# One core, an mLSTM and differential-attention block: z of the odd heads and two gate blocks as three pairs with seven products each

## The chip, the core and the metric

The kernel runs on one core of a Trainium2 chip. The metric is the device time of one execution in microseconds (us), the median of several runs. PE is the engine of the matrix products (TensorE), DVE the vector engine, ACT the scalar engine, POOL is GpSimd, SP issues most DMAs.

## The reference

One layer over 1024 tokens of width 1024, all in float32. The input is normed (h), then projected with one wide matrix `w_in` into twelve segments:

```python
h = rmsnorm(x, norm_g[layer])
proj = jnp.einsum('bsd,de->bse', h, w_in[layer])
(a_q, a_k, a_v, a_o, a_z, a_g, b_q, b_k, b_v, b_z, g_a, g_b) = jnp.split(proj, _split_points(), axis=-1)
...
y_a = hm * jax.nn.sigmoid(a_o) * jax.nn.silu(a_z)
...
att = diff_attention(dq, dk, da_v, lam)
att = rmsnorm(att, da_subln_g[layer]) * (1.0 - lambda_init)
y_b = att.reshape(B, S, DA_WIDTH).astype(x.dtype) * jax.nn.silu(b_z)
...
mix = (jax.nn.sigmoid(g_a + gb[0]) * jnp.einsum('bsc,cd->bsd', y_a, w_branch_a[layer])
       + jax.nn.sigmoid(g_b + gb[1]) * jnp.einsum('bsc,cd->bsd', y_b, w_branch_b[layer]))
x = x + jnp.einsum('bsd,de->bse', mix, w_out[layer])
```

Branch A is a gated linear recurrence in chunks, in both directions, with 4 heads (hm). Branch B is attention with 8 heads; each head has two score matrices, softmaxes both, and takes one from the other times lambda. `b_z` has 128 columns for each head of branch B; `g_a` and `g_b` have 8 blocks of 128 columns each.

## The kernel before

Every float32 product is made of three passes: both operands are split into a high and a low part (names that end in H and L, `wH`, `wL`, `hH`, `hL`), and H*H, H*L and L*H are summed in PSUM.

The stages, in order of time: the start (norm, transposes of x, four blocks of gates with plain projections), to 68 us; the **pair stage**, to 398 us; the lead-in to attention (q and k of head 0, its z, and the values of heads 0 and 1), to 455 us; **attention** of 8 heads, to about 1120 us; branch A's recurrence (the ML stage); the last gates; the two branch products, the mix and the output.

*A plain projection* (`proj`, L415) takes a block of 128 columns of `w_in` and makes it for 1024 tokens in two halves of 512. Each half is 24 matmuls of 128x512 (8 blocks of the inner dimension, three passes), cut into 8 pieces of 3. One block is 48 matmuls.

*A pair* (`pair_units`, L270) makes two blocks of 128 columns for all tokens as a 2x2 product of halves with seven products (named f = 0 to 6) in place of eight. Each product is 4 inner blocks by three passes, 12 matmuls, so a pair has 84. `load_form` (L230) makes the seven weight forms from the two raw blocks: sums and differences on POOL (L243, L254), the H part on ACT (L262), the L part on DVE for f = 0, 4, 6 and on POOL for the others (L264). The operands of the other side (`TH`, `TL`) are made once and live until the stage ends. Three products share one PSUM bank, and ACT copies partial sums out of it (`u`, L298) before the next may be added. A *sink* takes the four results. There are 16 pairs: in groups of four, a pair of `ak` (with the convolution), one of `ao` and `az`, one of `aq` (convolution), one of `ao` and `az`. Raw blocks lie by turns in the pool of weights (even pairs) and in the stage's own pool (odd pairs). Work of branch A's scalar gates and of the rope tables is put in at fixed pairs (`more`).

*A head of attention* has 8 steps (`da_cycle`), a step being 128 query rows. Names below are tiles: score products `S` (12 matmuls of 64 rows, two score matrices, one PSUM buffer each); on DVE the two maxima `nm` (L926); on ACT the two exponentials `e` (L928); on DVE `r` and the combination `e` (L932 to L934). The result is transposed a step later, in two groups of four (`T`), copied as `pH` by ACT (L947) and `pL` by DVE (L948). Every second step has `PV`, 24 matmuls with the values, whose result ACT copies out as `att` (L961), and the other steps have the transposes of `att` for the squares. In steps 4 and 5 the head before is finished (`G`, L991): its `att` times z (`zg`) is scaled and stored. The transposes, PV, the squares and G share two PSUM buffers (tag `T`).

Into these steps other work is woven: the plain projections of q and k of the next head, with rope (`da_proj`, L842: `first` and `second`, DVE products, POOL sums and casts, then DMAs that spread the halves into `kst` and `qq`), the values of the next two heads (`da_v`), z of a head, and gate blocks (`fill`; how many for each head is in `FILL`, L38). The order is written by `Weaver` (L62) from costs and lags in a table (`LAG`, L42); PE then runs in that order, and the other engines in one that the framework's scheduler sets.

z of head h is 48 matmuls, a tanh on ACT (L880) and a product on DVE (L881). Of the 16 gate blocks 4 run at the start, 1 in head 0, 3 in head 7, 3 behind head 7, 2 in the ML stage, 3 after it.

Of the kernel before, what the change touches and what calls it, by code (L numbers as in the profile page):

```python
# [7 lines left out]
F32 = mybir.dt.float32  # L8
F32R = mybir.dt.float32r
I32 = mybir.dt.int32  # L10
AF = mybir.ActivationFunctionType
ALU = mybir.AluOpType
AX = mybir.AxisListType

S = 1024
# [3 lines left out]
NH_B = 8  # L19
# [15 lines left out]


INF = 1.0e9
FILL = (1, 0, 0, 0, 0, 0, 0, 3)  # L38
MM = 0.214
TP = 0.109  # L40

# [68 lines left out]
class Block:  # L110
# [202 lines left out]
    def oz_sink(self, i0):  # L313


        v, a, box = self.v, self.a, {}

        def sink(i, j, ps, rest):
            if "z" not in box:
                box["z"] = self.big("oz")  # L320
            z = box["z"][:, j * 512:(j + 1) * 512]
            first = j not in box
            box[j] = True
            if rest is not None:
                to = self.psA.tile([128, 512], F32, name="pj", tag="pj", bufs=2) if i == j == 1 else ps
                v.tensor_tensor(out=to, in0=ps, in1=rest, op=ALU.add)
                ps = to
            more = lambda out, x, y: v.scalar_tensor_tensor(out=out, in0=x, scalar=1.0, in1=y, op0=ALU.add, op1=ALU.mult)
            if i == 0:
                a.activation(out=z if first else ps, in_=ps, func=AF.Tanh, scale=0.5)  # L330
                if not first:
                    more(z, ps, z)
            else:
                th = self.s0.tile([128, 512], F32, name="tz", tag="tz", bufs=2)
                a.activation(out=th, in_=ps, func=AF.Tanh, scale=0.5)
                more(z if first else ps, th, ps)
                if not first:
                    more(z, z, ps)
            if not first:
                self.q.dma_start(out=self.gd_ml[i0][:, j * 512:(j + 1) * 512], in_=z)  # L340
        return sink

    def conv_sink(self, seg, n):

# [497 lines left out]
    def da_proj(self, h, st):  # L842
        A, v, a, p, q = self.A, self.v, self.a, self.p, self.q
        w1 = self.w1
        fb = lambda x: x.bitcast(F32)
        kA, kB = ("rope", h, 0), ("rope", h, 1)

        def first(half, pa):
            c = slice(half * 512, (half + 1) * 512)
            m = [w1.tile([128, 512], F32, name=f"m{i}", tag=f"m{i}", bufs=1) for i in range(2)]  # L850
            st["m"] = m
            v.tensor_tensor(out=m[0], in0=pa, in1=self.cosT[:, c], op=ALU.mult)
            v.tensor_tensor(out=m[1], in0=pa, in1=self.sinT[:, c], op=ALU.mult)

        def second(half, pb):
            c = slice(half * 512, (half + 1) * 512)
            if half == 0:
                st["k"] = w1.tile([128, 2, S], F32R, name="kst", tag="kst", bufs=2)
            qq = st["q", half] = w1.tile([128, 2, 512], F32R, name="qq", tag="qq", bufs=3)
            m = st["m"]  # L860

            hl = w1.tile([128, 4, 512], F32R, name="hl", tag="hl", bufs=1)
            v.tensor_tensor(out=fb(hl[:, 2]), in0=pb, in1=self.sinT[:, c], op=ALU.mult)
            v.tensor_tensor(out=fb(hl[:, 3]), in0=pb, in1=self.cosT[:, c], op=ALU.mult)
            p.tensor_tensor(out=m[0], in0=m[0], in1=fb(hl[:, 2]), op=ALU.subtract)
            p.tensor_tensor(out=m[1], in0=fb(hl[:, 3]), in1=m[1], op=ALU.add)
            for i in range(2):
                p.tensor_copy(hl[:, i, :], m[i])
                p.tensor_tensor(out=hl[:, 2 + i, :], in0=m[i], in1=fb(hl[:, i, :]), op=ALU.subtract)
            for x in range(2):  # L870
                for i, to in enumerate((st["k"][:, :, c], qq)):
                    for j in range(2):
                        r, g = 64 * j + 32 * x, 64 * (1 - i) + 32 * j
                        q.dma_start(out=fb(to[r:r + 32]), in_=fb(hl[g:g + 32, x::2]))

        kz = ("w_in", OFF["bz"] + 128 * h)

        def zz(half, ps):
            st["g", half] = g = w1.tile([128, 512], F32, name="zg", tag="zg", bufs=2)
            a.activation(out=g, in_=ps, func=AF.Tanh, scale=0.5)  # L880
            v.scalar_tensor_tensor(out=g, in0=g, scalar=1.0, in1=ps, op0=ALU.add, op1=ALU.mult)  # L881

        qk = []
        for half in range(2):
            qk += self.proj(kA, half, lambda ps, half=half: first(half, ps))
            qk += self.proj(kB, half, lambda ps, half=half: second(half, ps), name=("qk", h))
        z = self.proj(kz, 0, lambda ps: zz(0, ps)) + self.proj(kz, 1, lambda ps: zz(1, ps), name=("z", h))
        for half in range(2):
            z[(half + 1) * self.PIECES - 1].after = ((("G", h - 1, half), LAG["G"]),)
        return qk, z  # L890
# [538 lines left out]
    def build(self):  # L1429
# [19 lines left out]
        do = lambda f, cost=0.0: Unit(cost, f)  # L1449
        pool = lambda *x, **k: tc.tile_pool(*x, **k)  # L1450
        with pool(name="const", bufs=1) as self.const, \
# [16 lines left out]
            dt = lambda n: [self.dram.tile([128, S], F32, name=f"{n}{i}") for i in range(8)]  # L1468
            self.tg = {"ga": dt("tga"), "gb": dt("tgb")}
            self.ya, self.yb, self.gd_ml = dt("ya"), dt("yb"), dt("gm")  # L1470
            self.cd = {n: dt("c" + n) for n in ("ak", "akH", "akL", "aqH", "aqL")}
            self.pairs, sinks, self.praws, self.f = [], [], {}, {}
            for n in range(NH_A):
                for i, seg in enumerate(("ak", "aq")):
                    self.pairs.append(((seg, 2 * n), (seg, 2 * n + 1)))
                    sinks.append(self.conv_sink(seg, n))
                    self.pairs.append((("ao", 2 * n + i), ("az", 2 * n + i)))
                    sinks.append(self.oz_sink(2 * n + i))
            self.ident = self.const.tile([128, 128], F32, name="ident")
            make_identity(self.nc, self.ident)  # L1480
            self.mhalf = self.const.tile([128, 8], F32, name="mhalf")
            self.v.memset(self.mhalf, -0.5)

            gq = [("gb", i) for i in range(8)] + [("ga", i) for i in range(8)]
            fill = lambda m: sum((self.gate_units(*gq.pop(0)) for _ in range(m)), [])

            def begin():
# [15 lines left out]
            w = Weaver()  # L1503
# [40 lines left out]
            w.add(leave("ps0", "s0", "tf"), enter("w1", "w1", side="right"), banks("ps1", S=2, T=2))  # L1544
            w.banks.update(S=1, T=2)
            qk, z = zip(*[self.da_proj(h, sts[h]) for h in range(NH_B)])
            w.add(do(lambda: setattr(self, "ahead", True)), *qk[0], *z[0], *self.da_v(0, sts[0:2]))
            prev = None
            for h in range(NH_B):
                cur = self.da_parts(h, sts[h])  # L1550
                main = sum((self.da_cycle(cur, prev, t) for t in range(8)), [])
                ahead = qk[h + 1] if h + 1 < NH_B else []
                if h + 1 == NH_B:
                    nxt = fill(FILL[h]) + z[h]
                elif h % 2 == 1:
                    nxt = ahead + self.da_v((h + 1) // 2, sts[h + 1:h + 3]) + fill(FILL[h])
                else:
                    nxt = z[h - 1] + ahead + fill(FILL[h]) + z[h] if h else ahead + fill(FILL[0])
                w.weave(main, nxt)
                prev = cur  # L1560
            end = sum((self.da_cycle(None, prev, t) for t in range(6)), [])
# [79 lines left out]
```

## Time and profile before

| | us |
|---|---|
| median of three runs | 1701.33 (1698.94 to 1702.51) |
| the profiled execution | 1699.79 |
| its span, first to last instruction | 1698.0 |
| PE busy with matmuls | 1650.1 |
| DVE, ACT, POOL busy | 994.1, 760.0, 635.3 |

The profiled execution lies 1.5 us under the median. Times of rows are counted from the start of its span. A matmul of 512 columns shows a duration of about 0.39 us in a row, but the next one starts 0.23 us after it: the matmuls overlap, and what counts is the distance of the starts.

### The profile page before, as it was taken

The page shows a single profiled execution, that of the slowest core. Times are in us where ns is not written, and L with a number is a line of the kernel's source. Part 1 is how long each engine was busy: PE and PEld are TensorE (multiplying, and loading weights), DVE is VectorE, ACT ScalarE, POOL GpSimd, SP SyncE. Part 2 cuts the span into 40 slices and gives each one's busy share as a digit, 9 for nine tenths or more (in the row PEclk, how much of TensorE's full clock was granted, in tenths as well). Part 3 has the DMA queues.
Part 4 walks back from the last instruction along what each step waited for, and adds up shares of the span by engine and source line. Part 5 has one row for each costly group of instructions (what it writes and reads, how often), then busy time and mean ns, then how long its engine had stood idle before and what let it go on. Part 6 is the DMA issues. An engine that isn't in the chain of part 4 may idle for free. (4 is left out here: it accounts for less than half of the span.)

```text
span 1698.0 us, 25367 instructions
## 1 busy us (share of the span) xinstructions
PE 1650.1 (97%) x9431; PEld 1387.7 (82%) x9431; DVE 994.1 (59%) x1799; ACT 760.0 (45%) x1522; POOL 635.3 (37%) x712
## 2 busy tenths in 40 slices
PE   7999999999999999999999999999999898999998
PEld 5777887887888988898888888889999777888887
DVE  5778668674277666766666765126666644135533
ACT  6454555543254454454445454325656644022221
POOL 5767676665343235424351431221331311212000
PEclk9999999999999999999999999999999999999999
DMA  5334434434231213221230221175554327344222
GB/s 179 101 118 134 137 115 134 124 124 137 75 81 44 63 38 87 63 63 37 76 88 26 63 75 63 50 208 155 143 170 140 104 93 244 119 142 136 87 92 83
DMA packets 175630, 178.79 MB, mean 105 GB/s; under 512 B 12185, under 2 KB 135410, under 8 KB 175506
## 3 DMA queue, kind: packets, MB, share of 16 engines
q1 hardware_dynamic: 174594, 175.58, 34.5%
q8 instruction: 74, 1.21, 0.3%
q10 hardware_dynamic: 912, 1.59, 0.2%
q14 instruction: 50, 0.41, 0.1%
HBM read 114.11 MB, written 46.24 MB: 94 GB/s over the span
## 5 line engine op out<-in xcount | busy, mean ns | idle before, releaser
L429 PE MATMUL pj<-hH,wH 128*128 128x512 f32 x640 | 266.3, 416 | 3.3 <-ACT f L542 1.5
L429 PE MATMUL pj<-hH,wL 128*128 128x512 f32 x640 | 251.9, 394 | 1.7 <-POOL wL L207 1.7
L429 PE MATMUL pj<-hL,wH 128*128 128x512 f32 x640 | 250.6, 392 | 0.2 <-DVE hL L580 0.2
L209 POOL TENSOR_TENSOR wL<-raw,wH 128x1024 fp32r<-128x1024 f32 x41 | 99.6, 2429 | 284.2 <-ACT wH L204 281.8
L928 ACT ACTIVATE e<-S,nm 128x1024 f32<-128x1024 f32 x128 | 142.7, 1115 | 134.2 <-DVE nm L926 133.9
L948 DVE TENSOR_TENSOR pL<-T,pH 128x512 fp32r<-128x512 f32 x128 | 87.9, 688 | 117.4 <-ACT pH L947 116.7
L926 DVE TENSOR_REDUCE nm<-S 128x1 f32<-128x1024 f32 x128 | 150.5, 1217 | 10.1 <-PE S L923 9.3
L429 PEld LDWEIGHTS pj<-hH,wH 128*128 128x128 f32 x640 | 120.7, 189 | 37.8 <-issue 14.4
L451 PE MATMUL pj<-wH,hH 128*128 128x256 f32 x512 | 149.9, 293 | 1.6 <-DVE vL L1035 1.3
L451 PE MATMUL pj<-wL,hH 128*128 128x256 f32 x512 | 144.9, 283 | 1.4 <-POOL wL L207 1.4
L429 PEld LDWEIGHTS pj<-hH,wL 128*128 128x128 f32 x640 | 120.4, 188 | 30.1 <-POOL wL L207 3.1
L451 PE MATMUL pj<-wH,hL 128*128 128x256 f32 x512 | 144.5, 282 | 0.0
L429 PEld LDWEIGHTS pj<-hL,wH 128*128 128x128 f32 x640 | 121.0, 189 | 18.2 <-DVE hL L580 0.6
L429 PE MATMUL pj<-sl_yb,wH 128*128 128x512 f32 x384 | 121.8, 397 | 4.7 <-ACT sl_yb L1314 2.1
L947 ACT CAST pH<-T 128x512 fp32r<-128x512 f32 x128 | 74.7, 584 | 100.5 <-PE T L131 99.9
L204 ACT CAST wH<-raw 128x1024 fp32r<-128x1024 f32 x56 | 58.8, 1050 | 126.8 <-PE pj L429 86.4
L923 PE MATMUL S<-kst,qq 64*128 64x512 f32 x768 | 106.5, 408 | 0.0
L451 PEld LDWEIGHTS pj<-wH,hH 128*128 128x128 f32 x512 | 97.7, 191 | 6.8 <-issue 3.9
L451 PEld LDWEIGHTS pj<-wL,hH 128*128 128x128 f32 x512 | 97.5, 190 | 2.3 <-POOL wL L207 2.3
L451 PEld LDWEIGHTS pj<-wH,hL 128*128 128x128 f32 x512 | 97.7, 191 | 0.1
L429 PEld LDWEIGHTS pj<-sl_yb,wH 128*128 128x128 f32 x384 | 73.3, 191 | 22.8 <-DVE sl_yb L1315 3.3
L934 DVE SCALAR_TENSOR_TENSOR e<-e,r,e 128x1024 f32<-128x1024 f32 x64 | 88.8, 1388 | 2.2
(358 smaller groups left out, 4099.9 us busy)
## 6 DMA issues: line engine op xcount, KB each, us to landing
raw<-in_w_in_dram SPq DMA_DIRECT2D x88, 512.0 KB, 3.8
kst<-hl SPq DMA_DIRECT2D x64, 128.0 KB, 2.4
qq<-hl SPq DMA_DIRECT2D x64, 128.0 KB, 2.4
x<-in_x_dram SPq DMA_DIRECT2D x8, 512.0 KB, 6.2
cak<-y SPq DMA_DIRECT2D x16, 256.0 KB, 2.3
cakH<-cin SPq DMA_DIRECT2D x16, 256.0 KB, 4.4
cakL<-tz SPq DMA_DIRECT2D x16, 256.0 KB, 4.0
gm<-oz SPq DMA_DIRECT2D x16, 256.0 KB, 2.8
```

What stands on the lines that cost most here:

```text
L204: self.a.copy(wH, raw)
L209: self.p.tensor_tensor(out=wL, in0=raw, in1=wHf, op=ALU.subtract)
L429: self.t.matmul(ps, lhsT=l[:, k, :], rhs=r, start=(n == 0), stop=(n == 23))
L451: self.t.matmul(ps[:, i, :], lhsT=l, rhs=r[:, k, :], start=(kh == 0 and k == 0 and m == 0), stop=(kh == 1 and k == 3 and m == 2))
L923: self.t.matmul(ps[:, o], lhsT=qq[r, x, c], rhs=k[r, y, o], start=(m == 0), stop=(m == 2))
L926: v.tensor_reduce(out=nm, in_=ps, axis=AX.X, op=ALU.max, negate=True)
L928: a.activation(out=e, in_=ps, func=AF.Exp, bias=nm[:, 0:1], accum_out=Z[:, j, t:t + 1])
L934: v.scalar_tensor_tensor(out=e0, in0=e, scalar=r[:, 0:1], in1=e0, op0=ALU.mult, op1=ALU.add)
L947: a.copy(pH[:, :, s], ps)
L948: v.tensor_tensor(out=pL[:, :, s], in0=ps, in1=pH[:, :, s].bitcast(F32), op=ALU.subtract)
```

## The change

Six blocks move from plain projections into pairs: z of heads 1, 3, 5 and 7 (two pairs) and the blocks 4 and 5 of branch B's gate (one pair). The new pairs stand behind the fourth pair of the groups 0, 1 and 2, so there are 19. Their sinks write z (with its tanh and product) and the gate to DRAM. In attention, an odd head loads its z from there into the same buffers `zg` (`load_z`, after the last G of the head before). Even heads keep the plain projection of z, now alone beside the next head's q and k. z of head 0 moves from the lead-in into head 0, in the place of a gate block. Head 7 has two gate blocks in place of three and its z. The cast of the rotated q and k on GpSimd, which the words for the change name, stands in the kernel before too (L868); the diff has no line of it.

```diff
-FILL = (1, 0, 0, 0, 0, 0, 0, 3)
+FILL = (0, 0, 0, 0, 0, 0, 0, 2)
...
+    def stored_sink(self, to, finish):
+        box = {}
+        def sink(i, j, ps, rest):
+            if i not in box:
+                box[i] = self.big("out")
+            out = box[i][:, j * 512:(j + 1) * 512]
+            if rest is not None:
+                sums = self.psA.tile([128, 512], F32, name="pj", tag="pj", bufs=2) if i == j == 1 else ps
+                self.v.tensor_tensor(out=sums, in0=ps, in1=rest, op=ALU.add)
+                ps = sums
+            finish(out, ps, i)
+            self.q.dma_start(out=to[i][:, j * 512:(j + 1) * 512], in_=out)
+        return sink
...
+    def z_sink(self, heads):
+        def finish(out, ps, i):
+            self.a.activation(out=out, in_=ps, func=AF.Tanh, scale=0.5)
+            self.v.scalar_tensor_tensor(out=out, in0=out, scalar=1.0, in1=ps, op0=ALU.add, op1=ALU.mult)
+        return self.stored_sink([self.gz[h] for h in heads], finish)
...
+        def load_z(half):
+            st["g", half] = g = w1.tile([128, 512], F32, name="zg", tag="zg", bufs=2)
+            q.dma_start(out=g, in_=self.gz[h][:, half * 512:(half + 1) * 512])
+
+        if h % 2 == 1:
+            return qk, [Unit(0.0, lambda half=half: load_z(half)) for half in range(2)]
...
+                if n < 3:
+                    blocks = (("gb", 4), ("gb", 5)) if n == 0 else (("bz", 4 * n - 3), ("bz", 4 * n - 1))
+                    self.pairs.append(blocks)
+                    sinks.append(self.gate_sink(blocks) if n == 0 else self.z_sink([h for _, h in blocks]))
...
-            gq = [("gb", i) for i in range(8)] + [("ga", i) for i in range(8)]
+            gq = [("gb", i) for i in (0, 1, 2, 3, 6, 7)] + [("ga", i) for i in range(8)]
...
-            w.add(do(lambda: setattr(self, "ahead", True)), *qk[0], *z[0], *self.da_v(0, sts[0:2]))
+            w.add(do(lambda: setattr(self, "ahead", True)), *qk[0], *self.da_v(0, sts[0:2]))
...
-                    nxt = fill(FILL[h]) + z[h]
+                    nxt = fill(FILL[h])
                 elif h % 2 == 1:
-                    nxt = ahead + self.da_v((h + 1) // 2, sts[h + 1:h + 3]) + fill(FILL[h])
+                    nxt = ahead + self.da_v((h + 1) // 2, sts[h + 1:h + 3])
                 else:
-                    nxt = z[h - 1] + ahead + fill(FILL[h]) + z[h] if h else ahead + fill(FILL[0])
+                    nxt = ahead + z[h]
+                if h % 2 == 1:
+
+                    k = [i for i, u in enumerate(main) if u.name and u.name[0] == "G"][-1] + 1
+                    main[k:k] = z[h]
```

(`gate_sink`, left out, is `z_sink` with the gate's tanh alone, on ACT, and the gate's tiles in DRAM.)

The first place is PE in head 7, step 6, from its score products on (`pj` are projections, `att` the squares' transposes, `e` the transposes of the probabilities). Before:

```order
L923 MATMUL S<-kst,qq 128x512 x12
L429 MATMUL pj<-hH_170,wH 128x512
L429 MATMUL pj<-hL_172,wH 128x512
L429 MATMUL pj<-hH_170,wL 128x512
...
L429 MATMUL pj<-hH_170,wL 128x512
L131 MATMUL T<-ident,att 128x128 x2
L131 MATMUL T<-ident,e_10211 128x128 x4
```

After, from the last transposes of step 5 to the score products of step 7:

```order
L131 MATMUL T<-ident,e_10280 128x128 x8
L960 MATMUL S<-kst,qq 128x512 x12
L131 MATMUL T<-ident,att 128x128 x2
L131 MATMUL T<-ident,e_10360 128x128 x8
L960 MATMUL S<-kst,qq 128x512 x12
```

All projections have gone from between the score products of steps 6 and 7 (21 matmuls in the kernel before).

The second place is ACT in head 7 after the change, steps 5 to 7, two rows of `e` for each step:

```order
L965 ACTIVATE e_10360,Z<-S,nm 128x1024
L965 ACTIVATE e_10364,Z<-S,nm 128x1024
L998 COPY att<-T 128x256
L984 CAST pH<-T 128x4x128 x2
L1008 ACTIVATE T,ms<-T 128x128 x2
L984 CAST pH<-T 128x4x128
L965 ACTIVATE e_10441,Z<-S,nm 128x1024
L965 ACTIVATE e_10445,Z<-S,nm 128x1024
L984 CAST pH<-T 128x4x128
L965 ACTIVATE e_10486,Z<-S,nm 128x1024
L965 ACTIVATE e_10490,Z<-S,nm 128x1024
L998 COPY att<-T 128x256
```

In steps 5 and 7 `att`, which empties the PSUM buffer of PV, stands behind both exponentials; `pH` of the second group of step 6 stands behind those of its step.

The third place is DVE in the lead-in, from the rope products of the second half of head 0 on (`m` and `hl` are those products, `vL` the low part of the values). Before:

```order
L852 TENSOR_TENSOR m_3767<-pj,cosT 128x512
L853 TENSOR_TENSOR m_3768<-pj,sinT 128x512
L881 SCALAR_TENSOR_TENSOR zg<-zg,pj 128x512
L863 TENSOR_TENSOR hl<-pj,sinT 128x512
L864 TENSOR_TENSOR hl<-pj,cosT 128x512
L881 SCALAR_TENSOR_TENSOR zg<-zg,pj 128x512
L903 TENSOR_TENSOR vL<-pj,vH 128x256 x8
```

After:

```order
L883 TENSOR_TENSOR m_4196<-pj,cosT 128x512
L884 TENSOR_TENSOR m_4197<-pj,sinT 128x512
L940 TENSOR_TENSOR vL<-pj,vH 128x256
L894 TENSOR_TENSOR hl<-pj,sinT 128x512
L895 TENSOR_TENSOR hl<-pj,cosT 128x512
L940 TENSOR_TENSOR vL<-pj,vH 128x256 x7
```

Both z products are gone, and one `vL` now stands ahead of the last two rope products.

## Rows read from the trace of the kernel before

**Rows 1.** The page's part 1: busy time, share of the span, instructions of each engine.

```profile
PE 1650.1 (97%) x9431; PEld 1387.7 (82%) x9431; DVE 994.1 (59%) x1799; ACT 760.0 (45%) x1522; POOL 635.3 (37%) x712
```

**Rows 2.** Busy times by stretch: PE, PEld, DVE, ACT, POOL; granted clock, DMA share, GB/s.

```profile
68.00:398.00 330.00, 325.22 (x1406) 257.17 (x1405) 241.46 (x366) 174.69 (x315) 220.98 (x197) 1.00 0.41 126
398.00:432.40 34.40, 32.99 (x146) 27.00 (x145) 9.13 (x14) 4.01 (x6) 18.24 (x14) 1.00 0.42 121
432.40:455.50 23.10, 23.10 (x193) 23.00 (x192) 3.23 (x7) 5.00 (x11) 4.52 (x5) 1.00 0.20 46
455.60:518.40 62.80, 62.80 (x375) 49.85 (x374) 47.33 (x63) 32.94 (x65) 25.62 (x22) 1.00 0.31 81
991.90:1067.00 75.10, 75.10 (x447) 60.79 (x447) 45.55 (x60) 38.51 (x79) 16.29 (x16) 1.00 0.18 57
```

**Rows 3.** PE timeline in the lead-in: start, duration, instruction, idle before it.

```profile
426.87 0.50 PE L429 MATMUL pj<-hH,wH 128*128 128x512 f32 x1 [1.41 <-DVE zg L881]
```

**Rows 4.** Who PE waited for in the pair stage: total, times, longest.

```profile
PE T L291 <- ACT u L298: 3.1, 4, 1.1
```

**Rows 5.** ACT and DVE timeline in the lead-in.

```profile
426.74 0.68 DVE L863 TENSOR_TENSOR hl<-pj,sinT 128x512 f32<-128x512 f32 x1
427.34 0.68 DVE L864 TENSOR_TENSOR hl<-pj,cosT 128x512 f32<-128x512 f32 x1
...
438.40 0.37 ACT L902 CAST vH<-pj 128x256 fp32r<-128x256 f32 x1 [4.31 <-PE pj L451]
...
438.81 0.42 DVE L903 TENSOR_TENSOR vL<-pj,vH 128x256 fp32r<-128x256 f32 x1 [4.50 <-ACT vH L902]
```

**Rows 6.** Timeline of one score step (head 7, step 5): PE, DVE, ACT.

```profile
1041.68 1.66 PE L923 MATMUL S<-kst,qq 64*128 64x512 f32 x12
1043.27 0.65 PE L131 MATMUL T<-ident,rb_y 128*128 128x128 f32 x4
...
1043.37 2.36 DVE L926 TENSOR_REDUCE nm<-S 128x1 f32<-128x1024 f32 x2 [0.27 <-PE S L923]
...
1045.82 1.11 ACT L928 ACTIVATE e<-S,nm 128x1024 f32<-128x1024 f32 x1
1046.84 0.19 ACT L928 ACTIVATION_READ_ACCUMULATOR e<-S,nm 128x1 f32 x1
...
1047.06 0.16 DVE L932 RECIPROCAL r<-Z 128x1 f32<-128x1 f32 x1 [0.67 <-ACT e L928]
...
1047.57 1.28 DVE L934 SCALAR_TENSOR_TENSOR e<-e,r,e 128x1024 f32<-128x1024 f32 x1
```

**Rows 7.** PE timeline: score products of head 0, steps 2 to 5.

```profile
470.73 1.65 PE L923 MATMUL S<-kst,qq 64*128 64x512 f32 x12
...
478.19 1.65 PE L923 MATMUL S<-kst,qq 64*128 64x512 f32 x12
...
486.42 1.65 PE L923 MATMUL S<-kst,qq 64*128 64x512 f32 x12
...
494.12 1.66 PE L923 MATMUL S<-kst,qq 64*128 64x512 f32 x12
```

**Rows 8.** Groups by line: busy us, mean ns of one, idle time before.

```profile
L948 DVE TENSOR_TENSOR pL<-T,pH 128x512 fp32r<-128x512 f32 x128 | 87.9, 688 | 117.4 <-ACT pH L947 116.7
L961 ACT COPY att<-T 128x256 f32<-128x256 f32 x32 | 11.9, 372 | 51.7 <-PE T L959 51.6
L868 POOL CAST hl<-m 128x512 fp32r<-128x512 f32 x32 | 25.3, 798 | 0.8
```

**Rows 9.** Busy times by stretch, columns as in rows 2, around a stall in the ML stage.

```profile
1353.00:1357.40 4.40, 0.49 (x2) 0.14 (x1) 2.25 (x11) 0.88 (x2) 0.00 (x0) 0.99 0.41 121
1357.40:1362.00 4.60, 4.53 (x20) 3.96 (x21) 0.83 (x3) 1.17 (x3) 0.69 (x2) 0.64 0.54 171
```

**Rows 10.** PE timeline behind that stall.

```profile
1358.60 0.63 PE L429 MATMUL pj<-hH,wL 128*128 128x512 f32 x1
1359.02 0.63 PE L429 MATMUL pj<-hH,wH 128*128 128x512 f32 x1
```

More of the change, by code (lines that the diff above doesn't have):

```diff
@@ L341, in oz_sink, with gate_sink, finish @@
         return sink
+    def stored_sink(self, to, finish):
[11 more added lines that the diff above has]
+        return sink
+    def gate_sink(self, blocks):
+        idx = [(0 if seg == "ga" else 8) + i for seg, i in blocks]
+        def finish(out, ps, i):
+            self.a.activation(out=out, in_=ps, func=AF.Tanh, scale=0.5, bias=self.gbh[:, idx[i]:idx[i] + 1])
+        return self.stored_sink([self.tg[seg][i] for seg, i in blocks], finish)
+    def z_sink(self, heads):
+        def finish(out, ps, i):
+            self.a.activation(out=out, in_=ps, func=AF.Tanh, scale=0.5)
+            self.v.scalar_tensor_tensor(out=out, in0=out, scalar=1.0, in1=ps, op0=ALU.add, op1=ALU.mult)
+        return self.stored_sink([self.gz[h] for h in heads], finish)
     def conv_sink(self, seg, n):
@@ L1470, in build @@
             self.ya, self.yb, self.gd_ml = dt("ya"), dt("yb"), dt("gm")
+            self.gz = {h: self.dram.tile([128, S], F32, name=f"gz{h}") for h in range(1, NH_B, 2)}
             self.cd = {n: dt("c" + n) for n in ("ak", "akH", "akL", "aqH", "aqL")}
```

## The prediction, made before the change was run

> **What bounds the kernel now.** I read the page's busy times first: the matmuls of PE fill 97% of the span, no other engine over 59% [rows 1]. The busy times by stretch then show where the change acts [rows 2]: the pair stage (68 to 398 us) has 4.8 us without a matmul, the projections of head 0 (398 to 432.4) have 1.4 us, the value products behind them and all of the attention none: in the stretch of head 0 PE is busy for 62.8 of 62.8 us, in that of head 7 for 75.1 of 75.1. So every matmul taken out is worth its full interval, but only as long as other matmuls cover the softmax chain. That chain is the second thing to read, in the rows of one score step [rows 6]. Seen from the start of its score products (1041.68), the two maxima on DVE end at 4.05 us, the second exponential on ACT at 5.25 (its sum by 5.35), and DVE has the combined row ready at 7.17. A next score product needs both S buffers, so it can't start before about 5.3 us, whatever PE has to do.
>
> **Part by part.** *Products removed.* Six blocks of 48 matmuls leave the attention and its lead-in: z of heads 1, 3, 5, 7 and two gate blocks (the z of head 0 only moves, into the place of the gate block that head 0 had). That is 288 matmuls. The lead-in gives (34.4 - 1.4) / 146 = 0.226 us each [rows 2]; the pair stage, 1376 full matmuls and some 2.5 us of small ones in 325.2 us, gives 0.2345. I take 0.229, nearer to the first, which is the same instruction: **-66.0 us** (ends -65.1 and -67.5). With z of head 0 the wait of 1.41 us ahead of its second bank also goes [rows 3]: **-1.4**.
>
> *Products added.* Three pairs with 7 products of 12 matmuls are 252 matmuls at 0.2345: 59.1 us. The 16 pairs of now have 4.8 us of waits, mostly for ACT copying a partial sum [rows 2, 4], 0.3 each, and a new pair has the same copies: **+60.0** (ends: 57.0 at 0.226 with no wait, 62 with a wait of the 1.1 us kind in each new pair). Their casts and differences on ACT, DVE and POOL have cover: a new pair has the weight forms that a pair of o and z has, no convolution, and these engines are busy for 53 to 73% of that stage [rows 2]. Raw weights, stores of z and loads of z are DMA beside it: DMA's share there is 0.41.
>
> So far: -7.4 us. If nothing else happened, the change would be worth this. Now what loses its cover.
>
> *Lead-in.* On DVE the first vL of the value products now stands ahead of the last two rope products, which free the bank that the second value block waits for. The first block ends 48 x 0.12 = 5.76 us after its start. Then vH on ACT (0.37), vL on DVE (0.42, started 0.41 after vH [rows 5]) and two rope products of 0.69 that follow each other at 0.6 come one behind the other: 0.2 + 0.4 + 0.4 + 0.6 + 0.7 = **+2.3** (ends 0 and 3). In the kernel of now they ran before it. The first score product should still wait for nothing: from the end of the rope products (428.0 [rows 5]) to it (455.6 [rows 2]) there are 28 us now, for POOL's sums and casts (of 0.8 us [rows 8] and up) and the DMAs of q and k; 17 us stay.
>
> *Heads 2, 4, 6.* They have now what head 0 has today, one z block and the next rope, in 62.8 us without a wait [rows 2]. One place is thinner: in score step 7 PE has S, 3 matmuls, the 24 of PV and 8 transposes. From the starts of steps 2, 3 and 4 of head 0 (lengths 7.46, 8.23, 7.70, with 21, 12 and 21 projection matmuls of 0.226 in them) [rows 7] I get S with 8 transposes 2.7, with the squares' transposes 2.9, with PV 5.5; so 6.2 here. The last four transposes need the bank that PV leaves, and ACT empties it (att, 0.37 [rows 8]) behind the second exponential (5.35) and the new tanh of z (0.6): 6.35, and 0.35 for the transposes make 6.75. Wait 0.57, three times: **+1.7** (ends 0 and 3).
>
> *Head 7.* The weave spends both gate blocks in steps 0 to 4; steps 5, 6, 7 have none left (six blocks' worth of filler stood there and before, now two). Step 5: S, PV, 8 transposes (5.5) and G's four transposes (0.65 by their row [rows 6], about 0.4 without the overlap with what follows) are 5.9 us of work; att again stands behind the exponential, 5.35 + 0.4 + 0.4 = 6.2, wait 0.3. Step 6: work 2.9 us, but its first maximum waits on DVE until the row of step 5 (7.17) and two pL (0.69 each [rows 8], overlapping a little) are through, at 8.4, which is 2.2 after its start; 2.36 for both maxima and 1.1 for the exponential make 5.8: wait 2.9. Step 7: work 5.5; one more pL, the row of step 6 and the last pL put its first maximum at 2.45, the second exponential's end at 6.1, att at 6.5, the last transposes at 6.9: wait 1.4. Together **+4.6** (ends 2.4, where only the exponential's 5.3 in step 6 counts, and 8).
>
> *At nothing:* the two loads of z sit on SP behind the store of the head before, whose completion they wait for (its buffers are the ones they fill). Queued behind them are weights and q and k of the next head, used a head later. GpSimd's cast is no change: the cast of rotated q and k already runs on POOL, 32 of them [rows 8], and no line of the diff touches it. The ML stage and the output keep their order.
>
> **Sum:** -66.0 - 1.4 + 60.0 + 2.3 + 1.7 + 4.6 = **+1.2 us**. The profiled execution took 1699.8 us, so 1701.0 by its own time; the median of the three runs is 1701.3, so I forecast **1702.5**, no change that can be told: about 0.2% (3.4 us) is what a measurement of this kernel tells from none.
>
> **Rivals.** *The waits are smaller (faster).* If ACT reaches att ahead of the second exponential, and pair waits don't grow, what is left is the chain itself in step 6 (2.4) and the lead-in (2.3): -67.4 + 59.1 + 4.7 = -3.6, 1697.7. Without any wait it would be -8.3, 1693.0. For it: head 0 shows that the same filler covers a whole head [rows 2]. Against: ACT takes its instructions in the built order, and att stands behind both exponentials in all four places.
>
> *The waits of head 7 slow PE itself (slower).* At 1353 to 1357.4 us PE has 0.49 us of work in 4.4 us, and then the granted clock is 0.64 for 4.6 us, full matmuls 0.43 apart in place of 0.23: the level of 1.2 GHz [rows 9, 10]. Steps 6 and 7 of head 7 would have gaps of about 2.6 and 1.7 us with 8 to 10 transposes around them. If the clock falls after each, S (1.6 us) doubles in step 7 and the projections behind it (9 matmuls, 2.1 us) too: +1.6 + 2.1, with the sum 1.2 + 3.7 = +4.9, 1706.2. It decides if the granted clock falls at all there: the stretch at 1353 was emptier than these, and a single wait of 1.4 us at 425 left it at 1.00 [rows 2, 3]. The Trainium skill ("TensorE: Matmul & The Clock Gate", section on HAM oscillation) says that waits between short bursts of matmuls let the clock fall back to half and that each fall is paid again; the row at 1357.4 agrees with 0.64, and by that rule this rival's 1706.2 is the time.
>
> *The change does not do what its words say.* True for GpSimd's part, worth 0, and contained in the sum.
>
> **How the numbers follow.** The forecast's case has 0.52: its terms are read from rows, but six of them stand against each other, and the pair stage's order shifts with every new pair. Smaller waits 0.25, slower clock or as much in more pair waits 0.23. The forecast's case lies within 1699 to 1705; to 1695.5 it takes in most of the rival without waits, to 1709 the clock with waits of the pairs at their upper end. Faster by over 0.2%: 0.25; within: 0.52; slower: 0.23.
>
> **What would show it.** Right: PE has 9395 matmuls for 9431; the pair stage is 59 to 61 us longer; from the first score product to the last it is some 45 us shorter than now (33 of products less in heads 2, 4 and 6, 16 less in head 7 up to its last score product, less 5 of waits); DVE's vL ahead of the rope products with a PE wait of 2.3 us before the second value block; steps 5 to 7 of head 7 at about 6.2, 5.8 and 6.9 us. Wrong: step 6 of head 7 under 5 us, which the chain excludes; a wait of several us at the change from pairs to attention (rope weights late, since the last pair now holds their buffers); a clock under 1.00 in head 7; waits of the new pairs over 3 us in all.

## The result, and the profile after

The changed kernel takes 1703.91 us in the median of 22 executions (1700.74 to 1706.14), the kernel before, measured beside it, 1698.96 (22 executions). The ratio is 1.0024, 95% interval [1.0018, 1.0031]: the change is some 4 us slower, and nearly all of the interval lies beyond the 0.2% that the prediction takes as the least that can be told from no change. Measured again (**change_again**, below), the ratio was 1.0034 [1.0022, 1.0046].

The profiled execution of the changed kernel is among its shortest: 1700.83 us, span 1699.0. Against the span of the kernel before's profile (1698.0) that is +1.0 us, close to the +1.2 of the forecast's sum. So there are two things to explain: how this difference comes about (partly by chance, as the part on the prediction shows), and why most executions take 3 us more than the profiled one. Busy times (page, part 1; to be read against [rows 1]):

```profile
PE 1645.9 (97%) x9395; PEld 1382.6 (81%) x9395; DVE 1008.9 (59%) x1817; ACT 772.3 (45%) x1546; POOL 657.5 (39%) x730
```

9395 matmuls, 36 fewer, as forecast. Busy times by stretch, columns as in [rows 2]; the stretches are the pair stage, the lead-in in two parts, head 0, and head 7 in three parts (steps 0 to 4, steps 5 to 7 with the last score products, what follows up to the ML stage):

```profile
67.40:455.30 387.90, 384.02 (x1659) 304.71 (x1658) 262.36 (x395) 199.12 (x357) 254.26 (x221) 1.00 0.39 122
455.30:480.00 24.70, 24.70 (x123) 20.96 (x123) 5.52 (x9) 3.21 (x4) 12.24 (x9) 1.00 0.55 163
480.00:502.40 22.40, 20.24 (x168) 19.91 (x166) 3.70 (x8) 3.89 (x9) 8.13 (x8) 1.00 0.21 50
502.40:565.00 62.60, 62.60 (x373) 49.86 (x372) 48.20 (x64) 32.78 (x65) 25.69 (x22) 1.00 0.30 76
1011.20:1053.30 42.10, 42.10 (x255) 33.85 (x254) 29.97 (x39) 23.11 (x49) 8.30 (x11) 1.00 0.18 57
1053.30:1068.60 15.30, 12.30 (x82) 9.00 (x82) 12.16 (x16) 9.31 (x20) 3.66 (x2) 0.95 0.26 87
1068.60:1125.20 56.60, 55.31 (x324) 48.12 (x321) 9.33 (x14) 16.22 (x33) 14.64 (x35) 0.98 0.33 98
```

The pair stage lost 3.9 us to waits with 19 pairs (4.8 before with 16). Head 0 is still full. The end of head 7 has 12.30 us of PE work in 15.30 us, and its granted clock is below 1.00, which no part of the attention had before.

Who PE waited for, from the first score product to the ML stage (total, times, longest). In the kernel before, the same view of 455.6 to 1122 us has no line at all:

```profile
PE T L131 <- ACT T L1008: 2.4, 3, 1.4
PE T L131 <- ACT att L998: 2.0, 4, 0.6
PE S L960 <- ACT e L965: 1.7, 2, 1.1
PE T L127 <- ACT kwH L1118: 1.3, 1, 1.3
PE T L131 <- DVE pL L985: 0.9, 2, 0.8
```

The first line is step 0 of heads 2, 4, 6 (transposes behind the squares' activations), the second step 7 of these heads (0.58 each) and step 5 of head 7, the third and fifth are steps 6 and 7 of head 7; the fourth, at the start of the ML stage, stood behind the 1122 us in the kernel before too. PE's timeline there (start, duration, instruction, idle before it):

```profile
1053.34 1.66 PE L960 MATMUL S<-kst,qq 64*128 64x512 f32 x12
...
1059.48 0.66 PE L131 MATMUL T<-ident,e 128*128 128x128 f32 x4 [0.25 <-ACT att L998]
1060.07 1.67 PE L960 MATMUL S<-kst,qq 64*128 64x512 f32 x12
1062.52 0.44 PE L131 MATMUL T<-ident,att 128*128 128x128 f32 x2 [0.78 <-DVE pL L985]
1063.12 1.35 PE L131 MATMUL T<-ident,e 128*128 128x128 f32 x8 [0.16 <-DVE pL L985]
1065.56 0.49 PE L960 MATMUL S<-kst,qq 64*128 64x512 f32 x1 [1.08 <-ACT e L965]
1066.65 2.58 PE L960 MATMUL S<-kst,qq 64*128 64x512 f32 x11 [0.60 <-ACT e L965]
1069.16 0.58 PE L996 MATMUL T<-pH,vH 128*128 128x256 f32 x1
1069.54 0.41 PE L996 MATMUL T<-pL,vH 128*128 128x256 f32 x1
1069.75 0.41 PE L996 MATMUL T<-pH,vL 128*128 128x256 f32 x1
...
1070.56 0.28 PE L996 MATMUL T<-pH,vH 128*128 128x256 f32 x1
1070.68 0.28 PE L996 MATMUL T<-pL,vH 128*128 128x256 f32 x1
```

Four waits of 2.6 us in all stand between 1060 and 1067 us. Behind them the eleven score products take 2.58 us (twelve took 1.67 a step earlier), and the first PV products follow at 0.21 in place of 0.12. The busy times by stretch show the clock beside it:

```profile
1060.10:1065.60 5.50, 3.44 (x24) 2.10 (x23) 5.50 (x6) 3.11 (x9) 0.68 (x1) 1.00 0.17 50
...
1067.10:1070.50 3.40, 3.40 (x17) 2.47 (x14) 3.37 (x5) 0.31 (x1) 0.00 (x0) 0.50 0.00 0
1070.50:1075.00 4.50, 4.47 (x34) 4.02 (x34) 3.10 (x6) 3.64 (x7) 0.44 (x2) 1.00 0.01 2
```

A clock of 0.50 is the 1.2 GHz level. This is the mechanism of the slower rival, in its place. The Trainium skill ("TensorE: Matmul & The Clock Gate", section on HAM oscillation) says that waits between bursts of matmuls let the clock fall back. These rows agree that it falls behind waits; the page's example has single waits of several us, and here the longest of the four is 1.08 us.

**Where the mean clock points.** For each execution the mean granted clock of its span is known. The 22 executions of the changed kernel have 0.9933 in the mean; 15 of them have 0.991 to 0.993 and a median of 1704.1 us, the 7 with 0.994 to 0.996 one of 1701.7. The kernel before has 0.9951 to 0.9954 in the mean of each of three later measurements. If PE is busy in the slow stretches, a mean clock c costs up to (1 - c) times the span: 11.4 us now, about 8.0 before, 3.4 more. This is an estimate, since the two clocks come from different measurements. Taken from the 5.0 us between the medians it leaves 1.6 that the clock doesn't account for.

### The profile page after: what moved, and what is told of

Read it like the earlier page. It is cut to its first block, busy times and chain, and to the rows that moved or that the text cites. A ratio compares the mean times of both kernels' runs of the same rounds, so it can differ in the third digit from the quotient of the medians.

```text
span 1699.0 us, 25419 instructions
## 1 busy us (share of the span) xinstructions
PE 1645.9 (97%) x9395; PEld 1382.6 (81%) x9395; DVE 1008.9 (59%) x1817; ACT 772.3 (45%) x1546; POOL 657.5 (39%) x730
## 5 line engine op out<-in xcount | busy, mean ns | idle before, releaser
L460 PE MATMUL pj<-hH,wH 128*128 128x512 f32 x544 | 227.1, 417 | 1.9 <-ACT f L573 1.5
L460 PE MATMUL pj<-hH,wL 128*128 128x512 f32 x544 | 214.0, 393 | 1.8 <-POOL wL L207 1.8
L460 PE MATMUL pj<-hL,wH 128*128 128x512 f32 x544 | 213.0, 392 | 0.2 <-DVE hL L611 0.2
L209 POOL TENSOR_TENSOR wL<-raw,wH 128x1024 fp32r<-128x1024 f32 x35 | 85.2, 2433 | 231.7 <-ACT wH L204 224.2
L460 PEld LDWEIGHTS pj<-hH,wH 128*128 128x128 f32 x544 | 102.4, 188 | 32.2 <-issue 13.8
L460 PEld LDWEIGHTS pj<-hH,wL 128*128 128x128 f32 x544 | 102.3, 188 | 26.1 <-POOL wL L207 3.3
L460 PEld LDWEIGHTS pj<-hL,wH 128*128 128x128 f32 x544 | 102.8, 189 | 15.7 <-DVE hL L611 0.6
L204 ACT CAST wH<-raw 128x1024 fp32r<-128x1024 f32 x50 | 52.5, 1050 | 136.6 <-PE pj L460 109.4
L291 PE MATMUL T<-TH,wL 128*128 128x512 f32 x304 | 102.5, 398 | 3.5 <-ACT u L298 2.9
L291 PE MATMUL T<-TH,wH 128*128 128x512 f32 x304 | 102.9, 398 | 0.0
```

The source lines that it names most:

```text
L204: self.a.copy(wH, raw)
L209: self.p.tensor_tensor(out=wL, in0=raw, in1=wHf, op=ALU.subtract)
L291: self.t.matmul(ps, lhsT=l[:, k, :], rhs=r[:, k, :], start=(first and k == 0 and m == 0), stop=(k == 3 and m == 2), skip_group_check=not f ...
L460: self.t.matmul(ps, lhsT=l[:, k, :], rhs=r, start=(n == 0), stop=(n == 23))
```

## The experiments

Three theories were tried. First: the thin steps at the end of head 7 lose it, by waits and by the clock behind them. Second: the pairs and the even heads lose it. Third: the clock is lost in the stages behind attention, which the change doesn't touch.

**spread7**: same instructions as the change, another order of PE in head 7. Its 32 filler pieces (of 3 projection matmuls each) are dealt out over all eight steps.

```diff
                     nxt = fill(FILL[h])
+                    steps = [t for t, n in enumerate((7, 2, 6, 2, 5, 2, 6, 2)) for _ in range(n)]
+                    for u, t in zip(nxt, steps):
+                        u.after = ((("S", h, t), 0.0),)
```

> The changed kernel with one thing different: the 32 filler pieces of head 7 (two gate blocks, 3 matmuls a piece) are tied to its score steps, 7, 2, 6, 2, 5, 2, 6, 2 of them to steps 0 to 7, where the change has none in steps 5 to 7. Same instructions, other order of PE in head 7. First theory (the change lost by the thin steps of head 7: some 4.6 us of waits by the forecast's sum, of which the trace of the changed kernel shows 2.5 us, and the fall of the granted clock to half that the trace shows there): the steps 5 to 7 show waits under 0.5 us each, no stretch at half clock in head 7, and the time is 3 to 6 us under the changed kernel, so 1698 to 1701. Second theory (the three pairs and the even heads lost it): head 7 gives 1 to 2 us at most, 1702 to 1703. Third theory (clock lost in the stage behind attention, as in the kernel before): no difference beyond 1 us, and the mean granted clock stays at 0.991 to 0.995.

1697.84 us (11 executions), ratio to before 0.9991 [0.9982, 1.0000]: 6 us under the change, a little more than the first theory expected. The waits of steps 5 and 6 have gone, and the score products of step 7 take 1.65 us:

```profile
1054.10 1.65 PE L960 MATMUL S<-kst,qq 64*128 64x512 f32 x12
...
1061.12 1.65 PE L960 MATMUL S<-kst,qq 64*128 64x512 f32 x12
...
1067.04 0.60 PE L131 MATMUL T<-ident,e 128*128 128x128 f32 x4
1068.21 0.55 PE L131 MATMUL T<-ident,e 128*128 128x128 f32 x3 [0.58 <-ACT att L998]
```

From head 7's first score product to the ML stage it has 109.6 us where the change has 114.0, so 4.4 us less in the profiles. (Their spans differ by 2.3 us only: behind attention the profile of spread7 is 2.6 us longer, with 6.9 us more at half clock there.) Over its 11 executions the mean clock is 0.9951, that of the kernel before. The second theory (2 us at most) and the third (no difference) fall for the bulk of the loss: with head 7's order alone the change is no longer slower than the kernel before.

**z_only, gate_only**: the change with the two z pairs alone (gate blocks plain, `FILL[7]` 4, so head 7 is full), and with the gate pair alone (z plain as before, `FILL[7]` 1 beside z). The line that picks the pairs in z_only; in gate_only it is `if n == 0`:

```diff
-                if n < 3:
+                if 0 < n < 3:
...
```

> The changed kernel with only its two pairs of z; the two gate blocks go back to plain projections, and head 7 has four of them, so it is as full as in the kernel before. By the forecast's terms: 192 matmuls at 0.229 out, -44.0; two pairs in, +40.0 (measured on the changed kernel 57.5 for three, so +38.3); the wait ahead of z -1.4, the lead-in +2.3, step 7 of heads 2, 4, 6 +1.7 (the trace of the changed kernel shows 2.4 more at their step 0). First theory (head 7 was what lost): -1.4 to +1 against the kernel before, so 1698 to 1700, no stretch at half clock in head 7. Second theory (pairs and even heads lost it): +2 to +4 against before, 1701 to 1703. Third theory (clock lost behind attention): as the changed kernel, +4 to +5.

> The changed kernel with only the pair of the two gate blocks; all z blocks are plain projections as in the kernel before, and head 7 has its z and one gate block, so it is as thin as in the changed kernel. By the forecast's terms: 96 matmuls at 0.229 out, -22.0; one pair in, +20.0 (measured 19.2); head 7 +4.6. First theory (head 7's thin steps and the clock lost there): +2 to +6 against the kernel before, 1701 to 1705, with waits in steps 5 to 7 and a stretch at half clock in or right behind head 7. Second theory (pairs and even heads): a third of the loss at most, 0 to +2. Third theory (clock lost behind attention): the same +4 to +5 whatever head 7 has.

1706.40 us, 1.0049 [1.0035, 1.0062], and 1707.62 us, 1.0055 [1.0042, 1.0067]. All theories missed both: parts of the change are slower than the whole. The place is the pair stage, 376.1 us and 357.9 us against 330.4, so 22.9 and 27.5 us a pair in place of 19.2. PE's timeline of the run with the z pairs:

```profile
286.64 0.31 PE L131 MATMUL T<-ident,gch 64*128 64x64 f32 x2 [1.67 <-DVE gc_sint L846]
...
288.60 0.63 PE L291 MATMUL T<-TH,wH 128*128 128x512 f32 x1
...
296.63 0.48 PE L291 MATMUL T<-hH,wL 128*128 128x512 f32 x1 [3.39 <-DVE gc_emt L846]
```

and DVE's, ahead of the second of these copies:

```profile
288.84 4.04 DVE L404 SCALAR_TENSOR_TENSOR pj<-cin,cols,pj 128x512 f32<-128x512 f32 x6
292.79 0.84 DVE L663 TENSOR_SCALAR wk<-wk 128x256 f32<-128x256 f32 x1
294.91 0.69 DVE L407 SCALAR_TENSOR_TENSOR y<-tz,pj 128x512 f32<-128x512 f32 x1 [1.28 <-ACT tz L405]
295.51 0.75 DVE L404 SCALAR_TENSOR_TENSOR pj<-cin,cols,pj 128x512 f32<-128x512 f32 x1
296.17 0.31 DVE L846 COPY gc_emt<-T 128x32 f32<-128x32 f32 x2
```

The gate columns of branch A (`gc`, put in at pair number 10, counted from 0) queue on DVE behind a convolution (L404, L407): pair 9 is now a pair of `ak`. In the kernel before pair 9 is `ao` and `az`, in the change it is z of heads 1 and 3, both without convolution. PE waits 1.7 and 3.4 us, and between them the clock is at half (columns as in [rows 2]):

```profile
288.10:291.50 3.40, 3.40 (x9) 2.15 (x8) 3.40 (x6) 0.62 (x1) 2.49 (x3) 0.50 0.66 175
```

The new theory was tried by moving that side work along with the pairs:

```diff
-                    more.setdefault((i + (k + step * j) // 14, (k + step * j) % 14), []).append(u)
+                    at = i + (k + step * j) // 14
+                    more.setdefault((at + (at >= 8) + (at >= 12), (k + step * j) % 14), []).append(u)
```

(**z_aligned**; in **gate_aligned** `at + (at >= 4)`.)

> The run with the two z pairs alone came out 7.3 us over the kernel before, and its trace has 5.1 us of waits and a stretch at half clock at 281 to 297 us, where the transposes of branch A's gate columns (put in at a fixed pair number, 10) now stand behind a pair with convolution; in the kernel before and in the change they stand behind a light pair. Here that side work is moved along with the pairs that it stood at before. If that placement is the cause: no wait above 1.3 us in the pair stage, its length 369 to 371 us (330.4 and two pairs of 19.2 to 20.0), and the whole at -2 to +1 against the kernel before, 1697 to 1700. If two pairs by themselves cost more than two thirds of three: still 375 us for the stage and +5 or more. The theory that the clock behind attention loses it would give +4 here too.

> The run with the gate pair alone, with branch A's side work moved along by one pair, as in the run before this one. If the placement caused its long pair stage (357.9 us): now 349.6 to 350.4 us, and the whole 7 to 8 us under that run, 1699.5 to 1701, which leaves +1 to +2 against the kernel before; that rest is head 7, thin as in the change (a wait of 1.4 us in its step 4, 0.4 to 0.8 in steps 6 and 7). If head 7's clock costs more than its waits show: +4 and a stretch at half clock in head 7. If the pair itself costs 27 us: no change.

The pair stage is 369.25 and 349.5 us: 19.4 and 19.1 a pair, the same as three pairs in the change (57.5 / 3 = 19.2). The whole is 1699.58, 1.0004 [0.9996, 1.0013], and 1701.36, 1.0013 [1.0004, 1.0021]. So a pair costs 19.2 us alone as well as with others, as long as the side work stands behind a light pair. The z half of the change by itself is worth nothing measurable, and the gate half, with its thin head 7, costs some 2 us; its profile has 3.4 us at half clock in that head.

**thin7**: the kernel before, with two gate blocks of head 7 moved behind attention.

```diff
-FILL = (1, 0, 0, 0, 0, 0, 0, 3)
+FILL = (1, 0, 0, 0, 0, 0, 0, 1)
...
+            w.add(*fill(2))
```

> The kernel before with two of the three gate blocks of head 7 moved to right behind attention, so that head 7 has its z and one gate block. No pair is added, PE has the same 9431 matmuls. First theory: head 7's last steps wait as in the changed kernel (2.5 to 4.6 us) and the granted clock falls there: +4 to +8 against the kernel before, 1703 to 1707, most of it between the first score product of head 7 and the end of the two moved blocks. Second theory (pairs and even heads lost it): +2.5 at most, 1699 to 1701.5, and no fall of the clock. Third theory: no difference that can be told in this stretch.

1701.31 us, 1.0015 [1.0006, 1.0024], some 2.5 us: below what the first theory expected, and all that the second allowed. Its head 7 waits 1.2 us in step 4 and 0.4 to 0.8 in steps 6 and 7, with one stretch at half clock (1029.8 us, 3.4 us), but over its 11 executions the mean clock is 0.9954, that of the kernel before. gate_aligned and gate_only have the same order in head 7, and waits of 0.42 and 1.22 us in step 4 like thin7. The score products behind these waits, in gate_aligned and in gate_only:

```profile
1048.20 3.17 PE L958 MATMUL S<-kst,qq 64*128 64x512 f32 x12
```

```profile
1056.96 2.10 PE L958 MATMUL S<-kst,qq 64*128 64x512 f32 x12
```

The first run has its 3.4 us at half clock here; the second has none in head 7, and its head 7 is 1.4 us shorter to the ML stage. So the same waits may or may not bring the fall, and a thin head alone costs its waits and little more; here z's 16 pieces still stand behind step 4. That the change pays more because its last three steps have nothing at all, and their waits follow one another, is argued from the rows and not tried by itself.

**bare7** takes that to its end: the change with no projection in head 7.

```diff
-FILL = (0, 0, 0, 0, 0, 0, 0, 2)
+FILL = (0, 0, 0, 0, 0, 0, 0, 0)
...
+            w.add(*fill(2))
             w.weave(end[:-2], fill(2))
```

> The changed kernel with the two gate blocks of head 7 moved to right behind attention: head 7 has no projection at all, the suspected cost taken to its end; PE has the same matmuls. Its steps then last as long as the softmax chain, 5.4 to 6.0 us each where they have 2.7 to 5.5 us of PE work, so 5 to 9 us of waits in the head in place of 2.5. If only the waits count: +3 to +6 against the change, 1707 to 1710, with the granted clock at 1.00 in most of the head. If the clock falls behind each of them, as it did behind step 6 of the change: several stretches at half clock, 10 to 25 us in all, and +8 to +18, 1712 to 1722. If head 7 has nothing to do with it: no difference beyond 2 us.

1716.15 us, 1.0102 [1.0089, 1.0116]: 11 to 13 us over the change, in the range expected with the clock and above the one for waits alone. Both contribute. The waits came out larger than expected: 9.9 us from head 7 to the ML stage where the change has 2.9, so some 7 us of the loss. The mean clock is 0.9908, and the profile has 29.5 us at half clock for 14.1 in the change's, of which 13.6 and 3.4 in head 7, so up to 5 us. The two stretches in head 7:

```profile
1057.10:1063.90 6.80, 6.57 (x28) 5.55 (x29) 4.99 (x8) 3.05 (x7) 0.44 (x2) 0.50 0.00 0
1016.20:1023.00 6.80, 6.22 (x27) 5.04 (x27) 4.69 (x7) 3.42 (x7) 0.00 (x0) 0.50 0.01 2
```

Behind other waits of the same head, of 0.9 and 0.6 us at 1030 us for one, the clock stayed at 1.00: it does not fall behind each.

**lead_in**: the change with a second buffer for the rope products.

```diff
-            hl = w1.tile([128, 4, 512], F32R, name="hl", tag="hl", bufs=1)
+            hl = w1.tile([128, 4, 512], F32R, name="hl", tag="hl", bufs=2)
```

> The changed kernel with one thing different: a second buffer for the rope products (hl), so that on DVE they stand ahead of the values' low parts again. Nothing in the attention changes. If the wait of 2.2 us before the second value block costs its length: -2.2 to -2.5 against the changed kernel, 1701.5 to 1703. If in the typical execution the clock also falls behind that wait (in one run with the same wait a stretch at half clock of 3.4 us followed it, in the profiles of the change none): -3 to -5, and a mean granted clock above the change's 0.991 to 0.993. If another wait takes its place: no difference.

1700.77 us, 1.0011 [1.0002, 1.0020]. In the profiles the lead-in is 44.7 us for 47.1, 2.4 less: the wait costs its length, the first case. The ratio to the kernel before is lower by 0.0013 than in the change's first measurement and by 0.0023 than in its second, 2.2 and 3.9 us, so these intervals don't tell whether the typical execution gains clock as well. Seven profiles have this wait of 2.16 us (the three of the change, spread7, z_only, z_aligned and bare7). In six of them the clock stays at 1.00 behind it; in z_aligned, where it stands before 466.57 us, the clock falls:

```profile
464.00:467.20 3.20, 1.04 (x9) 0.84 (x8) 1.99 (x4) 1.26 (x3) 1.20 (x1) 1.00 0.00 0
467.20:470.60 3.40, 3.40 (x18) 3.40 (x18) 0.00 (x0) 0.00 (x0) 3.34 (x5) 0.50 0.02 5
```

**change_again, change_third**: the changed kernel as it is.

> The changed kernel again, as it is, beside the others on the same chip. Its profiled execution so far (1700.8) lies 3 us under its median (1703.9), with a mean granted clock of 0.996, where 15 of 22 executions had 0.991 to 0.993. If the clock behind short stalls makes the difference, a profile with a mean of 0.993 shows about 24 us at half clock in place of 16, and they follow stalls in head 7 and in the stage behind it; median 1703 to 1705, 5 to 7 us over the run with head 7 spread. If head 7 is not the cause of it: half-clock stretches at 1355 and 1430 only, longer ones.

> The changed kernel once more, for its profile: both profiles so far were of executions of 1700.8 us, the others have a median of 1704 to 1705 at a mean granted clock 0.003 lower. If this one falls among the longer ones, it shows where they have their half-clock stretches: in head 7 by the first theory, behind attention by the third.

1705.34 us in the median of 5 (change_again), and a single 1701.57 (change_third). The profiled executions took 1700.75 and 1701.57, so both are short ones again; the four others of the first have clocks of 0.990 to 0.992 and 1705 us or more. The profile of change_again has twice the time at half clock in head 7:

```profile
1056.00:1063.60 7.60, 5.27 (x38) 3.51 (x36) 6.85 (x9) 5.02 (x14) 1.28 (x1) 1.00 0.36 124
1063.60:1070.40 6.80, 6.49 (x25) 4.95 (x26) 5.04 (x7) 3.42 (x6) 0.44 (x2) 0.50 0.00 0
```

No profile of one of the longer executions was had. That head 7 makes them long follows from spread7; at which instructions they spend their further half-clock time (their mean clock is lower by 0.003 and more, so some 10 us at half clock) stays open.

**spread_all**: spread7 and lead_in, and the 48 pieces of heads 2, 4 and 6 tied to their steps.

```diff
                     nxt = ahead + z[h]
+                    if h:
+                        steps = [t for t, n in enumerate((8, 4, 7, 5, 7, 4, 6, 7)) for _ in range(n)]
+                        for u, t in zip(nxt, steps):
+                            u.after = tuple(u.after) + ((("S", h, t), 0.0),)
```

> The changed kernel with the filler of head 7 tied to its steps, the 48 pieces of heads 2, 4 and 6 too (8, 4, 7, 5, 7, 4, 6, 7 to steps 0 to 7), and a second buffer for the rope products, so that on DVE they stand ahead of the values' low parts in the lead-in again. Against the run with head 7 alone (1697.8): the lead-in's wait of 2.2 us goes, and of the even heads' waits (0.58 in step 7, and 1.7, 0.3, 0.2 in step 0) most goes, 3 us: -4 to -5, 1693 to 1694, faster than both kernels. If those waits are hidden anyway, 1697 to 1698. The theory that puts the loss behind attention expects 1697 to 1698 too, since nothing there is changed.

1692.03 us (5 executions), 0.9959 [0.9947, 0.9971]: 6.7 us under the kernel before, so faster than it and than the change. Waits from the lead-in to the end of attention:

```profile
PE T L131 <- ACT T L1008: 1.1, 3, 0.8
PE T L131 <- ACT att L998: 0.8, 2, 0.6
```

Heads 2, 4 and 6 take 204.5 us together, for 208.3 in the change. So the saving of matmuls was real, and about what the part sum had as -7.4; the order spent it.

## Why the prediction was right, and where not

*The time.* 1703.9 lies in the range, 1.4 us over the forecast of 1702.5. Part of that nearness is luck. The forecast put its +1.2 us on a median of three runs, 1701.3, and the kernel before has 1698.96 over 22 executions, 2.4 us less. As a difference, forecast and result are +1.2 and some +4 us (5.0 between the medians), just past the line of 0.2% (the interval reaches down to 0.18%). The likeliest case was "no change that can be told" (0.52); what came is the slower rival (0.23, 1706.2), and with it one of the prediction's own signs of being wrong, a clock under 1.00 in head 7.

*Pair stage, +60.0.* It measured +57.5. The interval per matmul was right (PE's busy time there grew by 58.8 us for 59.1); the waits of 0.3 a pair that I added did not come (3.9 us in all, less than before). The aligned runs confirm 19.2 a pair. My reason for it, that a new pair has the copies of the others, missed what decides: which pair the side work stands behind. In the change that went well by the pairs' numbers; in the two runs with a part of it, it cost 7 and 8 us.

*Lead-in, -11.0 - 1.4 + 2.3 = -10.1.* It went from 57.3 to 47.1, -10.2, with a wait of 2.16 us where it was placed, and lead_in took it away.

```profile
484.95 0.38 PE L482 MATMUL pj<-wH,hH 128*128 128x256 f32 x1 [2.16 <-DVE hl L895]
```

*Heads 2, 4, 6, 33.0 of products less and +1.7, so -31.3.* They measured -27.3. Step 7 waits 0.58 us three times, as worked out (0.57; the sum there, 6.35 and 0.35, is 6.70, which gives 0.5). The term that was missing is step 0 of these heads, 1.4, 0.5 and 0.5 us behind the squares' activations: I had looked for thin places by counting PE's work a step, and this one has the work, but its transposes need a buffer that ACT frees late. The other 1.6 us are in no wait: without the waits, these heads lost 31.4 us for 144 matmuls, 0.218 each for the 0.229 assumed.

*Head 7, -22.0 + 4.6 = -17.4.* It measured -16.3 to the ML stage. Steps 5 and 6 are 6.73 and 5.49 us (forecast 6.2 and 5.8), with 0.25 and 2.0 us of waits (0.3 and 2.9). The 0.60 inside step 7's score products belongs to step 6's chain too: one matmul ran as soon as the first S buffer was free, the other eleven waited for the second exponential. That makes 2.6 of the 2.9; up to 0.9 of it comes from a slow combination that the forecast didn't have (last section), so the nearness is partly luck. Step 7's own wait (1.4) did not come. Its `att` waited for PE, whose work took longer at half clock, and not for the exponential:

```profile
1072.88 0.37 ACT L998 COPY att<-T 128x256 f32<-128x256 f32 x1 [0.30 <-PE T L996]
```

*The clock.* Here the weighing failed: I gave the forecast's case the most because the stretch at 1353 us was emptier, and a single wait of 1.4 us at 425 us had left the clock at 1.00 [rows 9, 2, 3]. Neither was of the kind that came, four waits within 7 us with work between them. The clock fell once there, behind the four, and not after each wait as the rival had it. The rival's price for it was 3.7 us; measured are up to 1.7 (half of 3.4 us) and 3.4 in the profiles, and 3.4 and 6.1 by the mean clocks of the two measurements against those of the kernel before.

*The sum.* I set the sum against one profiled execution, and that one came out as the sum says, +1.0 for +1.2. This is luck. The four parts above measured +57.5 - 10.2 - 27.3 - 16.3 = +3.7 in the profiles: the pair stage lies 2.5 under its term, the even heads 4.0 and head 7 1.1 over theirs. The remaining -2.7 comes from elsewhere, 2.0 of it from behind attention, which the change doesn't touch. There the profile of the kernel before has a wait of 1.33 us that the change's first profile doesn't have (its two others have 0.5 and 0.4), and twice the time at half clock around 1430 us. A row of PE's timeline in the kernel before, then that stretch in the kernel before and in the change (columns as in [rows 2]):

```profile
1147.63 0.35 PE L451 MATMUL pj<-wH,hH 128*128 128x256 f32 x1 [1.33 <-DVE vL L1035]
```

```profile
1429.00:1435.80 6.80, 5.94 (x13) 4.38 (x14) 3.17 (x4) 2.43 (x3) 0.00 (x0) 0.50 0.67 200
```

```profile
1432.30:1435.70 3.40, 3.09 (x7) 2.48 (x8) 1.82 (x3) 1.04 (x1) 0.00 (x0) 0.50 0.59 204
```

*The change doesn't do what its words say.* As far as GpSimd's cast goes this is true, and worth nothing, since no line of the diff touches it.

## What to carry to other kernels

When work that fills a wait-bound loop is taken out, what remains has to be dealt out over the steps anew: the same 32 and 48 pieces, spread by step (with a second buffer in the lead-in), turned +4 us into -7. Short waits can cost more than their length, because the clock may fall behind them, in some executions more than in others; so read the mean clock of all executions, not only the profiled one. A sum that agrees with one profiled execution is checked part by part, since errors and chance elsewhere can cancel. And side work that is put in at a numbered place must move when the numbers do.

## What was not expected of the hardware

How much time was spent at half clock in the same place differed from execution to execution of the same program: 3.4, 6.8 and 3.4 us in head 7 in three profiles. The Trainium skill ("TensorE: Matmul & The Clock Gate", Part 1) says of the start of a kernel that the number of slow matmuls varies by run; here the same is seen in the middle of one.

The combination on DVE takes 1.28 us [rows 6], but 2.16 when a product on POOL runs beside it. In head 7, step 5 of the changed kernel:

```profile
1059.50 1.28 POOL L1018 TENSOR_TENSOR zg<-att,zg 128x512 f32<-128x512 f32 x1 [3.23 <-ACT att L998]
```

```profile
1059.70 2.16 DVE L971 SCALAR_TENSOR_TENSOR e<-e,r,e 128x1024 f32<-128x1024 f32 x1
```

Of the 64 combinations in the changed kernel's profile, 20 took over 1.35 us, and in each of these a sum, difference, product or cast on POOL was running when it started. Another 12 have POOL work beside them and took 1.28 or 1.29 all the same; in these the POOL operation started later (or was one of under 0.3 us on small tiles). There it can be POOL that takes longer, as the same product does in head 2, behind a combination that started at 659.45 and took 1.28:

```profile
660.17 1.71 POOL L1018 TENSOR_TENSOR zg<-att,zg 128x512 f32<-128x512 f32 x1 [7.98 <-ACT att L998]
```

The combination of step 5 lies in the chain on which step 6 waited: the two pL and the maxima of step 6 stand behind it on DVE, so up to 0.9 us of step 6's wait come from it. The Trainium skill ("SBUF — State Buffer", section "SBUF: two separate sides") says that DVE operations with two operands in SBUF and GpSimd contend for one pair of ports and that the later one waits; these rows agree in both orders.
